# Most of the products with w1 and w3 of four feed-forwards as 2x2 blocks in seven products instead of eight

## The chip, the cores and the metric

One core of one Trainium2 chip runs one decoding step of a four-layer network in float32. The metric is the device time of one execution in microseconds; the median of the runs counts.

## The reference, cut to what matters

Each layer adds a token mixer and then a SwiGLU feed-forward to x. 512 prompt tokens and 8 x 4 sample tokens share the weights, which gives 544 columns. The mixers (convolution, latent attention, retention, convolution) are not changed. The feed-forward is:

```python
D_MODEL, D_FF, DEPTH, EPS = 1024, 2816, 4, 1e-6

def _rmsnorm(x, g):
    xf = x * lax.rsqrt(jnp.mean(x * x, axis=-1, keepdims=True) + EPS)
    return xf * g

def _swiglu(h, w1, w3, w2):
    return (jax.nn.silu(h @ w1) * (h @ w3)) @ w2

for i in range(DEPTH):
    ...                                            # x += mixer(rmsnorm(x))
    x = x + _swiglu(_rmsnorm(x, norm_ffn[i]), ffn_w1[i], ffn_w3[i], ffn_w2[i])
```

## The kernel before, in words

Activations are feature-major: x is 8 tiles (k = 0..7) of 128 features on the partitions by 544 columns, and a matmul takes half of the columns, 272. A float32 operand is split into a high and a low part (`wsplit`, lines 184 and 185, for weights: a cast on ScalarE, ACT in the rows, and a subtraction on VectorE, DVE in the rows; `split`, lines 191 and 192, for activations). A product is three matmuls: high by high, high by low, low by high. `gemm` (line 204) does this for one tile of 128 output features: 8 tiles of k, three parts, two halves of the columns, so 48 matmuls, into a pair of PSUM banks (`duo`, two of them).

`ffn` (line 428 on) works as follows. `enter` and `prep` (lines 224 and 225) make the split parts of x times the gain, without the division by the root mean square; that factor R needs a sum over all features (line 235) and some steps on ScalarE and VectorE (lines 246 to 250), and is multiplied onto each result (`times`, line 280). So the products may start before R is known. The 22 tiles of D_FF are walked in chunks of 8, 8 and 6. For each pair of tiles, 1 MB of w1 and 1 MB of w3 are loaded (`wload`, line 176, on SP's queue, into two buffers `raw`); for each tile, w1 is split and multiplied, then w3; silu (line 453) and the product of the two (line 456) follow, and the result is split into gh and gl. After a chunk, its part of w2 is multiplied with the chunk's g for all 8 tiles of x and added to x (`add_x`, line 284). In the last chunk of the last layer this is done by halves of the columns, with the final norm behind it (lines 473, 379 to 421).

What sets the order of the work: the code issues instructions into a planner (the Tile framework) that keeps dependencies, gives out buffers of the pools, and puts each engine's instructions into one fixed order when the program is built. Instructions of one engine that are ready in its plan run in the program's order; one whose inputs are late lets later ones pass. On the chip each engine then follows that fixed order. Six buffers `ws` hold three pairs of split weights; four scratch buffers `scr` and 16 buffers `xs` (split x) exist.

Of the kernel before, what the change touches and what calls it, by code (L numbers as in the profile page):

```python
# [70 lines left out]
def constants():  # L71
# [29 lines left out]
    # rows (batch, part, token) of the samples: high and low parts of keys and values, each with each  # L101
# [23 lines left out]
class Later:  # L125
    """a value whose instructions are issued at its first use"""
# [10 lines left out]
class Trunk:  # L137
# [4 lines left out]
    @contextmanager  # L142
    def in_order(self, *engines):
        """keeps what the block issues on these engines in its order"""
        tc, cur = self.tc, self.nc.cur_bb
        n = len(cur.bb.instructions)
        yield
        last = {}
        for i in cur.bb.instructions[n:]:
            if i.engine in engines:  # L150
                if i.engine in last:
                    tc.add_manual_dep(i, last[i.engine].name,
                                      mybir.DependencyInfo(mybir.DependencyClass.NoSync, mybir.DependencyReason.DATA),
                                      reason="order")
                last[i.engine] = i
# [6 lines left out]

    def bank(self, name):
        return self.psb.tile([P, 512], F, tag="b", name=name)

# [29 lines left out]
    def gemm(self, ps, wh, wl, xs, M=P, halves=(0, 1), order=None, then=None, hk=None):  # L195
        """ps[:M, half, :272] = sum_k w_k^T x_k"""
# [9 lines left out]

    def enter(self, gcol, order=range(KD), early=0):
        """hi and lo parts of x * g, and 1 / rms over the features"""
# [9 lines left out]
    def prep(self, xin, gcol, order=None):  # L218
        """hi and lo parts of x * g"""
        nc, out = self.nc, {}  # L220
        for k in order or range(len(xin)):
            hi = self.xsp.tile([P, T], FR, tag="xs", name="xh")
            lo = self.xsp.tile([P, T], FR, tag="xs", name="xl")
            nc.scalar.activation(hi, xin[k], AF.Copy, scale=gcol(k))
            nc.vector.scalar_tensor_tensor(out=lo, in0=xin[k], scalar=gcol(k), in1=hi[:, :].bitcast(F),
# [4 lines left out]
    def colsum(self, src):  # L230
        """sums over the partitions, on all of them, as two banks"""
# [7 lines left out]
    def rsqrt(self, v, y, t=None):  # L239
        """y = v ** -0.5"""  # L240
# [11 lines left out]
    def squares(self, xin, acc, order, first=True):  # L252
        """acc += the squares"""
# [10 lines left out]
    def rstat(self, xin, n, pool=None, tag="R", acc=None):  # L264
        """1 / rms over the features, on all partitions"""
# [24 lines left out]
    def run(self):  # L290
        tc, nc, A = self.tc, self.nc, self.A
        with ExitStack() as es:
# [5 lines left out]
            self.xsp = pool("xs", 16)  # L298
# [3 lines left out]
            self.psb = pool("psb", 4, space=bass.MemoryType.PSUM)  # L302
            self.x = self.cst.tile([P, KD, T], F, name="x")
            self.prologue()
            for l, kind in self.layers:
                if kind == 0:
                    self.conv(l, l // 3)
                elif kind == 1:
                    self.mla(l)
                else:  # L310
                    self.ret(l)
# [53 lines left out]
    def finish(self, ep, m, half):  # L365
        """the last norm and the turn to token-major of the m-th 128 features of a half of the tokens"""
# [42 lines left out]
    def last_norm(self, ep, e, half, tiles, t0, w):  # L409
# [3 lines left out]
        # (all rows of the samples' column are written)  # L413
# [14 lines left out]
    def ffn(self, l, last, order):  # L428
        tc, nc, A = self.tc, self.nc, self.A
# [3 lines left out]
        xs, R = self.enter(lambda k: self.col("norm_ffn", l * KD + k), order, EARLY)  # L433
        with ExitStack() as es:
            gp = es.enter_context(tc.tile_pool(name=f"ffn{l}", bufs=16))
            ep = es.enter_context(tc.tile_pool(name="end", bufs=1)) if last else None
            for f0, nf in ((0, 8), (8, 8), (16, 6)):
                gs = []
                for fp in range(0, nf, 2):
                    c0 = (f0 + fp) * P  # L440
                    r1 = self.wload(w1[:, :, c0:c0 + 256], KD, 256)
                    r3 = self.wload(w3[:, :, c0:c0 + 256], KD, 256)
                    for j in range(2):
                        wh, wl = self.wsplit(r1[:, :, j * P:(j + 1) * P], KD, P)
                        p1 = self.duo("p1")
                        self.gemm(p1, wh, wl, xs, order=order, then=R, hk=int(HK[0]))
                        R()
                        wh, wl = self.wsplit(r3[:, :, j * P:(j + 1) * P], KD, P)
                        p3 = self.duo("p3")
                        self.gemm(p3, wh, wl, xs, order=order)  # L450
                        t1 = self.scr("t1")
                        self.times(t1, p1, R)
                        nc.scalar.activation(t1, t1, AF.Silu)
                        t3 = self.scr("t3")
                        self.times(t3, p3, R)
                        nc.vector.tensor_mul(t3, t3, t1)
                        gs.append(self.split(gp, "g", t3, T))
                cuts = ((0, 256), (256, T)) if last and f0 + nf == FF // P else ((0, T),)
                late = None
                for half, (t0, t1) in enumerate(cuts):  # L460
                    for mp in range(0, KD, 2):
                        r2 = self.wload(w2[:, f0:f0 + nf, mp * P:(mp + 2) * P], nf, 256)
                        for j in range(2):
                            wh, wl = self.wsplit(r2[:, :, j * P:(j + 1) * P], nf, P)
                            if len(cuts) == 1:
                                ps = self.duo("p2")
                                self.gemm(ps, wh, wl, gs)
                                self.add_x(mp + j, ps)
                                continue
# [12 lines left out]
    def conv(self, l, j):  # L482
# [5 lines left out]
        with tc.tile_pool(name=f"cv{j}", bufs=1) as cp:  # L488
            # gated inputs: 30 rows of the past and 512 of the prompt; then 34 rows of each sample
# [11 lines left out]
            def taps_and_past():  # L501
# [7 lines left out]
                # tap 4 i + s of channel 32 g + c at partition 4 c + s  # L509
# [52 lines left out]
            # some channels tap by tap on VectorE  # L562
# [35 lines left out]
            # layer norm over the channels, about the mean of 128 of them  # L598
# [10 lines left out]
            def convolved(m, h):  # L609
                """a half of the tokens of a tile of channels, less K, and its part of the sums"""  # L610
# [32 lines left out]
            cs = [tuple(self.xsp.tile([P, T], FR, tag="xs", name="cs") for _ in range(2)) for _ in range(KD)]  # L643
# [982 lines left out]
```

## Time and profile before

| | us |
|---|---|
| median of 3 runs | 2868.93 |
| the three runs | 2868.93, 2869.55, 2865.14 |
| span of the profiled execution | 2899.4 |
| TensorE busy in it | 2836.5 (98%) |
| VectorE busy | 1563.7 (54%) |
| ScalarE busy | 991.3 (34%) |

The profiled execution is 1.1% longer than the median. Its instructions fill the span from the first to the last; the page shows nothing around it. A row of a view has a start or a mean duration in us or ns; on VectorE and ScalarE the next instruction can start a little before the one ahead of it has ended, so the step from start to start is what a full queue costs.

### The profile page before, as it was taken

To read this page: it belongs to the slowest core of one execution; us is meant where nothing else is said; L and a number is where in the kernel's file an instruction comes from. 1 tells how busy PE (TensorE), PEld (TensorE's weight loads), DVE (VectorE), ACT (ScalarE), POOL (GpSimd) and SP (SyncE) were. 2 spreads that over 40 slices of the span, in tenths; PEclk is the share of its full clock that TensorE was granted. 3 is DMA by queue.
4 is the path that set the end of the run, shared out by engine and by line. 5 is a ranking of instruction groups with operands and counts; after the bars stand their busy time and mean duration, and the time that the engine had idled before them with its cause. 6 is when DMAs were issued, how large, how long until landed. Compare 5 with 4: busy or idle time off the path is not lost.

```text
span 2899.4 us, 52901 instructions
## 1 busy us (share of the span) xinstructions
PE 2836.5 (98%) x23158; PEld 2662.8 (92%) x23158; DVE 1563.7 (54%) x2414; ACT 991.3 (34%) x1489; POOL 130.0 (4%) x217
## 2 busy tenths in 40 slices
PE   8989999999899999999999999999999999999998
PEld 7869999997679999999798897999999987999998
DVE  7875434356665434346656565743434796633335
ACT  4244222234454322224534344522223314422225
POOL 1000000012330000000101000000000000000000
PEclk9999999999999999999999999999999999999999
DMA  5453222233232222222524334322222444332323
GB/s 157 113 129 117 89 87 89 87 102 120 82 107 82 86 89 84 87 84 87 199 86 176 121 139 143 111 88 88 88 88 87 119 125 123 103 103 74 102 73 119
DMA packets 253116, 306.74 MB, mean 106 GB/s; under 512 B 14367, under 2 KB 217452, under 8 KB 252854
## 3 DMA queue, kind: packets, MB, share of 16 engines
q1 hardware_dynamic: 241260, 267.88, 29.8%
q0 software_dynamic: 11328, 33.59, 3.4%
q8 instruction: 182, 2.98, 0.4%
q10 hardware_dynamic: 298, 1.88, 0.2%
q14 instruction: 48, 0.39, 0.0%
HBM read 257.56 MB, written 24.01 MB: 97 GB/s over the span
## 4 chain that ended last, share of the span: by engine, by line
PE 94%; DMA 2%; SPq 1%; DVE 1%; ACT 1%; issue 1%; another core or an unknown queue 0%; ACTq 0%
PE p L204 54%; PE pg L204 7%; PE pqk L204 3%; PE pa L204 3%; PE pwo L204 3%; PE cv L621 2%; PE pw L204 2%; PE po L204 2%; PE pd L204 1%; PE pv L1273 1%; PE pv L1274 1%; PE pv L1275 1%; DMA S<-U 1%; PE ob L1508 1%; SPq L585 1%
## 5 line engine op out<-in xcount | busy, mean ns | idle before, releaser
L184 ACT CAST wh<-raw 128x1024 fp32r<-128x1024 f32 (+2 forms) x434 | 436.0, 1006 | 1458.0 <-PE p L204 1025.7
L204 PE MATMUL p<-xl,wh 128*128 128x272 f32 x2816 | 585.8, 290 | 0.0
L204 PE MATMUL p<-xh,wl 128*128 128x272 f32 x2816 | 583.4, 289 | 0.0
L204 PE MATMUL p<-xh,wh 128*128 128x272 f32 x2816 | 582.9, 289 | 0.0
L185 DVE TENSOR_TENSOR wl<-raw,wh 128x1024 fp32r<-128x1024 f32 (+2 forms) x434 | 506.3, 1168 | 94.5 <-ACT wh L184 71.4
L204 PEld LDWEIGHTS p<-xh,wh 128*128 128x128 f32 x2816 | 442.9, 188 | 0.7 <-DVE t L280 0.3
L204 PEld LDWEIGHTS p<-xh,wl 128*128 128x128 f32 x2816 | 443.5, 188 | 0.0
L204 PEld LDWEIGHTS p<-xl,wh 128*128 128x128 f32 x2816 | 441.4, 189 | 0.0
L280 DVE TENSOR_TENSOR t<-p,R 128x544 f32<-128x544 f32 x176 | 127.6, 725 | 570.8 <-PE p L204 570.7
L204 PE MATMUL p<-gl,wh 128*128 128x272 f32 x1312 | 273.0, 289 | 0.0
L204 PE MATMUL p<-gh,wl 128*128 128x272 f32 x1312 | 271.5, 288 | 0.0
L204 PE MATMUL p<-gh,wh 128*128 128x272 f32 x1312 | 271.4, 288 | 0.0
L284 DVE TENSOR_TENSOR x<-p,x 128x544 f32<-128x544 f32 x88 | 63.8, 725 | 279.6 <-PE p L204 279.6
L204 PEld LDWEIGHTS p<-gh,wh 128*128 128x128 f32 x1312 | 206.2, 188 | 0.0
L204 PEld LDWEIGHTS p<-gh,wl 128*128 128x128 f32 x1312 | 206.1, 188 | 0.0
L204 PEld LDWEIGHTS p<-gl,wh 128*128 128x128 f32 x1312 | 205.7, 189 | 0.0
L621 PE MATMUL cv<-S,W 128*32 128x240 f32 (+1 forms) x1408 | 100.1, 399 | 17.7 <-DMA S<-U 14.0
L204 PE MATMUL pg<-xh,wh 128*128 128x272 f32 x512 | 112.1, 295 | 4.1 <-ACT wh L184 4.1
L571 DVE SCALAR_TENSOR_TENSOR cc<-U,taps,cc 128x512 f32<-128x512 f32 (+1 forms) x180 | 113.3, 663 | 1.0
L204 PE MATMUL pg<-xh,wl 128*128 128x272 f32 x512 | 109.6, 292 | 0.0
L204 PE MATMUL pg<-xl,wh 128*128 128x272 f32 x512 | 108.4, 291 | 0.0
L621 PEld LDWEIGHTS cv<-S,W 128*32 128x32 f32 x1408 | 52.6, 115 | 59.5 <-DMA S<-U 23.6
(519 smaller groups left out, 4475.0 us busy)
## 6 DMA issues: line engine op xcount, KB each, us to landing
raw<-in_ffn_w SPq DMA_DIRECT2D x120, 1024.0 KB
raw<-in_conv_w_pw SPq DMA_DIRECT2D x28, 1024.0 KB
state<-in_state_ret SPq DMA_DIRECT2D x32, 512.0 KB
out_ret_state_sample<-state POOLq DMA_DIRECT2D x32, 512.0 KB
raw<-in_ffn_w SPq DMA_DIRECT2D x20, 768.0 KB
S<-U SPq DMA_DIRECT2D x48, 280.0 KB
raw<-in_ret_w_v SPq DMA_DIRECT2D x8, 1024.0 KB
raw<-in_ret_w_g SPq DMA_DIRECT2D x8, 1024.0 KB
```

What stands on the lines that cost most here:

```text
L184: self.nc.scalar.copy(hv, raw)
L185: self.nc.vector.tensor_sub(lv, raw, hv.bitcast(F))
L204: nc.tensor.matmul(ps[:M, h, :HF], lhsT=w[:, k, :], rhs=x[:, h * HF:(h + 1) * HF], start=(j == 0 and i == 0), stop=(j == n - 1 and i == 2))
L280: self.nc.vector.tensor_mul(self.v2(out), ps[:M, :, :HF], self.v2(R[:M, :]))
L284: self.nc.vector.tensor_add(x, ps[:, :, :HF], x)
L571: nc.vector.scalar_tensor_tensor(out=cc[m][:, a:z], in0=U[:, m, k + a:k + z], scalar=taps[:, m, k:k + 1], in1=cc[m][:, a:z], op0=ALU.mult, ...
L585: nc.sync.dma_start(S[:, g, a0 - c0:], bass.AP(src.tensor, src.offset, [list(src.ap[0]), [1, 4], [1, c1 - a0]]))
L621: nc.tensor.matmul(b[g * 32:(g + 1) * 32, :n], lhsT=W[:, g * 8 + i, :], rhs=S[:, g, 4 * i:4 * i + n], start=(i == 0), stop=(i == 7))
L1273: nc.tensor.matmul(out, lhsT=ah, rhs=bh, start=start, stop=False)
L1274: nc.tensor.matmul(out, lhsT=ah, rhs=bl, start=False, stop=False)
L1275: nc.tensor.matmul(out, lhsT=al, rhs=bh, start=False, stop=stop)
L1508: nc.tensor.matmul(s["ob"][q * 32:(q + 1) * 32, :], lhsT=s["qm"][:, e, q * 2 + r, :], rhs=ts[q // 2][:, q % 2, :], start=(q > 0 and r == 0 ...
```

## The change

The 22 tiles of w1 and w3 are now two tiles the old way (`plain`), then five quads of four tiles. In a quad, 512 output features by 1024 features of x by 544 columns are taken as 2x2 blocks: output halves of 256 features, halves of 512 in k, halves of 272 columns. Seven products of blocks (`product`, 24 matmuls each) replace eight (in effect 192 matmuls become 168 for each weight and quad). This is Winograd's form of Strassen's scheme: the weight blocks enter as themselves and as four sums (S, on VectorE, `whole`), each of the seven is split on its own; the blocks of x enter as themselves and as four differences (`less`), also split each on its own, once for a layer (`prepared`). The products are added up in PSUM where the accumulation allows it; three partial results for each weight are copied out by ScalarE (`kept`) and added on VectorE (`gate`, `value`).

Because sums of blocks are split into parts, R can't wait until after the product: x is multiplied with gain and R beforehand for the quads (`normed`, 16 operations of 272 columns), while `plain` still works as before. A quad's weights come as two loads of 1 MB for each of w1 and w3: the first 512 features of k into `raw`, the others into `raw2`, which has one buffer.

w2 now follows each quad (`down`): chunks of 6, 4, 4, 4, 4 tiles instead of 8, 8, 6. Two tiles of x are split and multiplied together, then added. Split x is kept in 8 pairs of buffers instead of 16 single ones, in all layers, and the PSUM pool of single banks is closed between mixer and feed-forward, where it serves as two pairs. Comments are taken out everywhere; nothing else of the mixers changes.

```diff
+            blocks, full = {}, {}
+            def block(dtype, name):
+                return bp.tile([P, 4, HF], dtype, tag="B", name=name, bufs=15)
+            def normed():
+                for j in range(4):
+                    full["B%d" % j] = block(F, "B")
+                r = R()
+                for k in range(KD):
+                    for h in range(2):
+                        hs = slice(h * HF, (h + 1) * HF)
+                        nc.vector.scalar_tensor_tensor(out=full["B%d" % (k // 4 * 2 + h)][:, k % 4, :], in0=self.x[:, k, hs],
+                                                       scalar=g(k), in1=r[:, hs], op0=ALU.mult, op1=ALU.mult)
+            def less(out, a, b):
+                full[out] = block(F, "T")
+                nc.vector.tensor_sub(full[out], full[a], full[b])
+            def parts(c, of):
+                blocks[c] = block(FR, "Bh"), block(FR, "Bl")
+                h, lo = blocks[c]
+                nc.scalar.copy(h, full[of])
+                nc.vector.tensor_sub(lo, full[of], flat(h))
+            def prepared():
+                normed()
+                parts("1", "B0")
+                less("T1", "B1", "B0")
+                less("T3", "B3", "B1")
+                parts("5", "T1")
+                less("T2", "B3", "T1")
+                less("T4", "B2", "T2")
+                for c, of in zip("63724", ("T2", "B3", "T3", "B2", "T4")):
+                    parts(c, of)
+            def weights(w, f):
+                r1 = self.rawp.tile([P, 2048], F, tag="raw", name="raw").rearrange("p (k c) -> p k c", k=4)
+                nc.sync.dma_start(r1, w[:, 0:4, f * P:f * P + 512])
+                r2 = bp.tile([P, 2048], F, tag="raw2", name="raw2").rearrange("p (k c) -> p k c", k=4)
+                nc.sync.dma_start(r2, w[:, 4:8, f * P:f * P + 512])
+                a11, a21, a12, a22 = r1[:, :, :256], r1[:, :, 256:], r2[:, :, :256], r2[:, :, 256:]
+                ...
+                def whole(op, a, b):
+                    t = self.xsp.tile([P, 1024], F, tag="xs", name="S").rearrange("p (k c) -> p k c", k=4)
+                    op(t, a, b)
+                    return t
+                def split(a):
+                    h, lo = ws("ah"), ws("al")
+                    nc.scalar.copy(h, a)
+                    nc.vector.tensor_sub(lo, a, flat(h))
+                    return h, lo
+                yield split(a11)
+                s1 = whole(nc.vector.tensor_add, a21, a22)
+                yield split(s1)
+                s2 = whole(nc.vector.tensor_sub, s1, a11)
+                yield split(s2)
+                yield split(whole(nc.vector.tensor_sub, a12, s2))
+                yield split(whole(nc.vector.tensor_sub, a11, a21))
+                yield split(a12)
+                yield split(a22)
+            def product(out, c, w, first, final):
+                wh, wl = w
+                bh, bl = blocks[c]
+                for t in range(2):
+                    m = slice(t * P, (t + 1) * P)
+                    for i, (a, b) in enumerate(((wh, bh), (wh, bl), (wl, bh))):
+                        for k in range(4):
+                            nc.tensor.matmul(out[:, t, :HF], lhsT=a[:, k, m], rhs=b[:, k, :],
+                                             start=(first and i == 0 and k == 0), stop=(i == 2 and k == 3),
+                                             skip_group_check=True)
+            def four(w, f, put):
+                ...
+                product(x2, "1", next(ws), True, False)
+                s1 = kept(x2, "u1")
+                x3 = self.pair("x3")
+                product(x3, "5", next(ws), True, False)
+                p5 = kept(x3, "p5")
+                product(x2, "6", next(ws), False, False)
+                u2 = kept(x2, "u2")
+                product(x3, "3", next(ws), False, True)
+                put("12", v(x3), u2)
+                product(x2, "7", next(ws), False, False)
+                put("22", v(x2), p5)
+                x1 = self.pair("x1")
+                product(x1, "2", next(ws), True, True)
+                put("11", v(x1), s1)
+                product(x2, "4", next(ws), False, True)
+                put("21", v(x2), None)
+                ...
+                def gate(which, ps, add):
+                    t = at(hidden[int(which[0]) - 1], which)
+                    if add is not None:
+                        nc.vector.tensor_add(t, ps, add)
+                        ps = t
+                    nc.scalar.activation(t, ps, AF.Silu)
+                def value(which, ps, add):
+                    t = at(hidden[int(which[0]) - 1], which)
+                    gh, gl = (at(x, which) for x in G[int(which[0]) - 1])
+                    if add is not None:
+                        v = self.scr("v").rearrange("p (t n) -> p t n", t=2)
+                        nc.vector.tensor_add(v, ps, add)
+                        ps = v
+                    nc.vector.tensor_mul(t, ps, t)
+                    nc.scalar.copy(gh, t)
+                    nc.vector.tensor_sub(gl, t, flat(gh))
+                four(w1, f, gate)
+                four(w3, f, value)
+            def down(f0, gs):
+                ...
+                        w = [self.wsplit(r2[:, :, j * P:(j + 1) * P], nf, P) for j in range(2)]
+                        if not ends:
+                            ps = [self.duo("p2") for j in range(2)]
+                            if mp == 0:
+                                for h in range(2):
+                                    for j in range(2):
+                                        self.gemm(ps[j], *w[j], gs, halves=(h,))
+                            else:
+                                for j in range(2):
+                                    self.gemm(ps[j], *w[j], gs)
+                            for j in range(2):
+                                self.add_x(mp + j, ps[j])
+                ...
+            plain(0, gs)
+            prepared()
+            f0 = 0
+            for f in range(2, FF // P, 4):
+                quad(f, gs)
+                down(f0, gs)
+                f0, gs = f + 4, []
```

## Rows read from the trace of the kernel before

**Rows 1.** The page: busy time of each engine, its share and instructions.
```profile
PE 2836.5 (98%) x23158; PEld 2662.8 (92%) x23158; DVE 1563.7 (54%) x2414; ACT 991.3 (34%) x1489; POOL 130.0 (4%) x217
```

**Rows 2.** Stretches of the first and last feed-forward: us, busy us (instructions) by engine, granted clock, DMA.
```profile
300.00:450.00 150.00, 150.00 (x1197) 150.00 (x1196) 58.32 (x67) 36.05 (x41) 0.00 (x0) 1.00 0.29 92
...
2550.00:2700.00 150.00, 150.00 (x1197) 150.00 (x1196) 58.93 (x66) 36.65 (x42) 0.00 (x0) 1.00 0.27 85
```

**Rows 3.** VectorE in time: start, duration, line; additions to x after 48 matmuls each.
```profile
346.71 0.72 DVE L284 TENSOR_TENSOR x<-p,x 128x544 f32<-128x544 f32 x1 [2.70 <-PE p L204]
...
352.74 0.72 DVE L284 TENSOR_TENSOR x<-p,x 128x544 f32<-128x544 f32 x1 [3.92 <-PE p L204]
```

**Rows 4.** TensorE in time: single-bank accumulation, three parts in turn.
```profile
229.26 0.29 PE L1273 MATMUL pw2h<-cs,wh 128*128 128x272 f32 x1
229.38 0.29 PE L1274 MATMUL pw2h<-cs,wh 128*128 128x272 f32 x1
229.51 0.29 PE L1275 MATMUL pw2h<-cs,wl 128*128 128x272 f32 x1
```

**Rows 5.** VectorE in time, a full queue: the steps of 544 and of 1024.
```profile
413.84 0.73 DVE L456 TENSOR_TENSOR t<-t,t 128x544 f32<-128x544 f32 x1
414.48 1.22 DVE L185 TENSOR_TENSOR wl<-raw,wh 128x1024 fp32r<-128x1024 f32 x1
415.61 0.72 DVE L192 TENSOR_TENSOR gl<-t,gh 128x544 fp32r<-128x544 f32 x1
```

**Rows 6.** Groups by shape: count, then busy us, mean ns of one, idle before.
```profile
L571 DVE SCALAR_TENSOR_TENSOR cc<-U,taps,cc 128x272 f32<-128x272 f32 x60 | 29.7, 495 | 0.3
L184 ACT CAST wh<-raw 128x1024 fp32r<-128x1024 f32 x373 | 391.1, 1050 | 1356.8 <-PE p L204 960.7 <-PE pg L204 81.7 <-PE pqk L204 64.7
L185 DVE TENSOR_TENSOR wl<-raw,wh 128x512 fp32r<-128x512 f32 x9 | 6.1, 683 | 1.1 <-ACT wh L184 0.7 <-issue 0.4
L191 ACT CAST gh<-t 128x544 fp32r<-128x544 f32 x88 | 57.1, 648 | 73.1 <-DVE t L456 71.4 <-issue 1.7
```

**Rows 7.** VectorE in time at the start of the first feed-forward: R's last step.
```profile
252.66 0.78 DVE L225 SCALAR_TENSOR_TENSOR xl<-x,vec,xh 128x544 fp32r<-128x544 f32 x1
253.36 0.72 DVE L250 SCALAR_TENSOR_TENSOR R<-rsq,R 128x544 f32<-128x544 f32 x1
```

**Rows 8.** The first two tiles' stretch in the four layers, columns as in rows 2.
```profile
242.80:267.70 24.90, 24.90 (x196) 24.57 (x195) 16.43 (x22) 14.98 (x21) 4.50 (x9) 1.00 0.41 130
935.60:960.50 24.90, 24.90 (x196) 24.74 (x195) 14.64 (x19) 11.61 (x14) 0.00 (x0) 1.00 0.28 86
...
2484.30:2509.20 24.90, 24.90 (x196) 24.57 (x194) 16.32 (x22) 14.66 (x20) 4.58 (x9) 1.00 0.40 130
```

**Rows 9.** One of those after R, columns as in rows 2.
```profile
254.00:268.00 14.00, 14.00 (x112) 13.83 (x111) 7.29 (x9) 6.20 (x7) 0.00 (x0) 1.00 0.46 150
```

**Rows 10.** TensorE in time after 4.1 us of idleness.
```profile
23.40 0.82 PE L204 MATMUL pg<-xh,wh 128*128 128x272 f32 x2 [4.11 <-ACT wh L184]
...
27.04 0.41 PE L204 MATMUL pg<-xl,wh 128*128 128x272 f32 x2
```

**Rows 11.** Stretches of latent attention around a lowered clock, columns as in rows 2.
```profile
705.00:709.60 4.60, 4.60 (x36) 3.54 (x35) 2.72 (x6) 1.49 (x4) 0.25 (x1) 1.00 0.17 57
709.60:716.40 6.80, 6.80 (x35) 4.01 (x36) 4.82 (x13) 4.47 (x11) 5.15 (x10) 0.50 0.40 131
```

**Rows 12.** SP's queue: one weight load's issue; then the stretch that holds its bytes.
```profile
319.30 0.37 SPq L176 DMA_DIRECT2D raw<-in_ffn_w  x1
320.00:324.00 4.00, 4.00 (x34) 4.00 (x33) 1.23 (x2) 1.59 (x2) 0.00 (x0) 1.00 0.83 262
```

**Rows 13.** TensorE in time: matmuls of two tiles mixed while x's parts come in.
```profile
249.26 0.54 PE L204 MATMUL p<-xh,wh 128*128 128x272 f32 x3
249.64 0.54 PE L204 MATMUL p<-xl,wh 128*128 128x272 f32 x3
```

**Rows 14.** The end of the program, columns as in rows 2.
```profile
2847.00:2889.00 42.00, 41.72 (x335) 41.09 (x333) 28.80 (x54) 27.31 (x53) 0.00 (x0) 1.00 0.35 120
```

More of the change, by code (lines that the diff above doesn't have):

```diff
@@ L161, in scr, with banks, pair @@
         return self.scrp.tile([P, T], F, tag="scr", name=name)
+    @contextmanager
+    def banks(self, duos=False):
+        with self.tc.tile_pool(name="psb", bufs=2 if duos else 4, space=bass.MemoryType.PSUM) as p:
+            self.psb, self.duos = p, duos
+            yield
     def bank(self, name):
+        if self.duos:
+            return self.pair(name)[:, 0, :]
         return self.psb.tile([P, 512], F, tag="b", name=name)
+    def pair(self, name):
+        return self.psb.tile([P, 2, 512], F, tag="b", name=name)
     def duo(self, name):
@@ L432, in ffn @@
         w2 = A["ffn_w2"][l].rearrange("(k p) c -> p k c", p=P)
-        xs, R = self.enter(lambda k: self.col("norm_ffn", l * KD + k), order, EARLY)
+        g = lambda k: self.col("norm_ffn", l * KD + k)
+        xs, R = self.enter(g, order, EARLY)
         with ExitStack() as es:
[L435 to L458, printed above, removed]
@@ new lines, in quad, with at @@
+            def quad(f, gs, between=None):
+                hidden = [self.xsp.tile([P, 2, T], F, tag="xs", name="hid") for _ in range(2)]
+                G = [pair_of_g() for _ in range(2)]
+                def at(x, which):
+                    return x[:, :, (int(which[1]) - 1) * HF:int(which[1]) * HF]
+                def gate(which, ps, add):
[16 more added lines that the diff above has]
+                four(w3, f, value)
+                for gh, gl in G:
+                    gs.extend((gh[:, j, :], gl[:, j, :]) for j in range(2))
@@ L459, in ffn @@
+            def down(f0, gs):
+                nf = len(gs)
+                ends = last and f0 + nf == FF // P
+                ep = None
+                if ends:
+                    qs.close()
+                    es.enter_context(self.banks())
+                    ep = es.enter_context(tc.tile_pool(name="end", bufs=1))
                 late = None
-                for half, (t0, t1) in enumerate(cuts):
+                for half, (t0, t1) in enumerate(((0, 256), (256, T)) if ends else ((0, T),)):
@@ new lines, in down @@
+                        if not ends:
[4 more added lines that the diff above has]
+                                        self.gemm(ps[j], *w[j], gs, halves=(h,))
+                            else:
+                                for j in range(2):
+                                    self.gemm(ps[j], *w[j], gs)
+                            for j in range(2):
+                                self.add_x(mp + j, ps[j])
+                            continue
@@ L641, in convolved @@
                 nc.vector.tensor_add(S2[:, hs], S2[:, hs], q)
-            cs = [tuple(self.xsp.tile([P, T], FR, tag="xs", name="cs") for _ in range(2)) for _ in range(KD)]
+            cs = [self.xpair("cs") for _ in range(KD)]
             def moments(h):
@@ L1135, in sample_products @@
                 def sample_products():
+                    ts = [t[:96, :512].bitcast(F) for _ in range(2) for t in self.xpair("tm")]
                     for c in range(3):
```

80 lines of the change are left out of this document (57 added, 23 removed).

## The prediction

> **What bounds the kernel now.** I read the page's busy times first [rows 1]: TensorE is busy 98% of the span, VectorE 54%, ScalarE 34%. An average hides stages, so the next view is the stretches inside the feed-forwards [rows 2]: there TensorE is busy all 150 of 150 us, at a granted clock of 1.00, while VectorE works 58 to 59 us and ScalarE 36. Nothing but matmuls sets the pace there, and a matmul taken away is time taken away, as long as VectorE and ScalarE, which the change loads, can follow. The pace: two additions to x that each end 48 matmuls start 6.03 us apart [rows 3], so a matmul of 272 columns costs 125.6 ns.
>
> **What is removed.** For each quad and weight 192 matmuls become 168. With two weights, five quads and four layers, 960 fewer: 960 x 0.1256 = 120.6 us. w2 keeps its count. The new products write twelve matmuls in a row into one bank where the old ones alternated between two; the single-bank accumulation of the convolution's last product runs at the same 0.12 to 0.13 us [rows 4], so I take the same pace.
>
> **VectorE and ScalarE in the quads.** A full VectorE queue steps 0.64 us for 544 columns and 1.13 for 1024 [rows 5]. One weight of a quad has four sums and seven subtractions of 1024 elements, 11 x 1.13 = 12.4 us. w1 adds three additions of 544 (1.9), w3 three additions, four products and four subtractions (7.0). So 14.3 and 19.4 us, beside 168 x 0.1256 = 21.1 us of TensorE each. `down` with four tiles: eight subtractions (0.68 [rows 6]) and eight additions to x (0.72 [rows 3]), 11.2 us beside 24.1. ScalarE has seven casts at 1.05, three copies and four functions at about 0.65 [rows 6]: 11.9 us beside 21.1. So no engine takes the place of TensorE on the average, but w3's half of a quad leaves VectorE only 1.7 us of slack. Three pairs of split weights let a split run two products, 6.0 us, ahead; its cast and subtraction need 2.2. That cover is why I cost the sums and splits of a running quad at nothing; if it is gone they cost what the third rival says.
>
> **The start of each feed-forward** is where the cover ends, and here the largest loss lies. The quads need R, and R's last step ends at 254.1 us in the first layer [rows 7]; the two old-style tiles end at 267.7 [rows 8] (the other three layers have the same stretch, 24.9 us). In the 14 us between, VectorE is already busy for 7.3 [rows 9], so 6.7 are free. The new block work: 16 multiplications of 272 columns at 29.7/60 = 0.495 us [rows 6], 7.9 us, and four differences and seven subtractions of 1088 elements, 11 x 1.13 x 1088/1024 = 13.2; in all 21.1 us. Since ready instructions go in program order, all of that stands ahead of the first weight's subtraction (1.2 us). So 21.1 + 1.2 - 6.7 = 15.6 us after the old-style tiles the first product can end; 16 of its 24 matmuls need only the high weight part and take 2.0 us of this, which leaves 13.6. The second product waits for its sum (1.13) and cast (1.05) while 1 us of the first is left: 1.2 more, 14.8. The least that the work allows: until the seventh product VectorE must do 21.1 + 12.4 + 1.9 - 6.7 = 28.7 us where TensorE would need 6 x 3.01 = 18.1, so 10.6 late in any order. The most, if the first product can't run ahead: 17.5. I take 14, nearer to program order, and 4 x 14 = 56 us; 42 to 70 for the range. TensorE stands still and has nothing else to run there.
>
> **After such a stop** TensorE doesn't resume at full pace: after 4.1 us of idleness the 16 matmuls from 23.40 to 27.04 took 3.64 us instead of 2.0 [rows 10], 1.6 lost. In latent attention the granted clock was 0.50, 1.2 of 2.4 GHz, for 6.8 us after a stretch in which TensorE had been busy in the trace at 36 matmuls in 4.6 us, thinner than in the feed-forward [rows 11]; half of that is 3.4 lost. I take 2 for each start, 8 us in all (0 to 14). The Trainium skill, "TensorE: Matmul & The Clock Gate", section "HAM oscillation — how this bites in real kernels", says that gaps in the matmul stream make the chip halve the clock, so that work after each gap starts slow. That speaks against this change, which puts four gaps into a stream that now has none; by it each start would lose the 3.4 us of the lowered stretch, and the sum would be 5.6 us worse.
>
> **Smaller terms.** The second load of a weight, `raw2`, has one buffer: w3's load can be issued only when w1's last split is done, in the fifth of seven products by the count of pairs. A load issued at 319.30 has moved its megabyte by 324 [rows 12], 4.7 us at most, and the first sum on it, cast included, is due about 9 to 10 us after the issue: it fits with some 2 us to spare, less when VectorE is behind. Behind it on SP's queue stands the next quad's load, behind the waiting sum on VectorE the additions that free PSUM. I take 0.4 us in each of the 20 quads, 8 us (0 to 40). `down` begins with the first half of the columns, whose blocks come last: product, cast and subtraction (0.72 + 0.65 + 0.72) behind the last matmul, with 6 ready matmuls (0.75 us) ahead in program order. The other half is ready, and the planner does mix matmuls of two results when one is late: runs of three instead of two in [rows 13]. So zero, and up to 20 x 1.4 = 28 us if it doesn't. At the program's end TensorE is busy 41.7 of 42 us with six tiles [rows 14]; with four, one tile of x for one half takes 1.5 us there and ScalarE needs about 1.4, so 2 us (0 to 4). The mixers' pairs of buffers and the PSUM pool that closes and opens: all old users are done about when the feed-forward starts; zero, at most 1 us for each of eight borders.
>
> **The sum.** 120.6 - 56 - 8 - 8 - 2 = 46.6 us less than the profiled 2899.4, which is its span. Scaled to the median of the runs (2868.93/2899.4): 46 us, so 2823 us.
>
> **Rivals.**
> First, the start is covered as well as the work allows: 42 instead of 56, no loss in the quads, clock or tail. Gain 120.6 - 42 = 78, so 2791 us. For it: ScalarE and TensorE have nothing in the way. Against: it needs weight sums to pass ready block work.
> Second, the quads limp: w3's half comes 2 us late each time because of the one buffer and the 19.4 of 21.1 us on VectorE. 40 instead of 8: gain 15, so 2854 us. For it: the small slack. Against: loads land in under 5 us, and `down` gives VectorE 13 us to recover.
> Third, slower: the plan doesn't run ahead. For five of seven products the chain is sum 1.13, cast 1.05, subtraction 1.13 = 3.3 us and two hand-overs between engines, against 3.0 us of a product. If splits start only one product ahead, each of the 280 products is late by some 0.4 us, 112 us: 2823 + 112 = 2935 us. The point from which it decides is 46/280 = 0.17 us for each product, little. Against it: three pairs, and sums that wait for nothing but a load.
> Fourth, the change doesn't bring the matmuls it says: 6720 matmuls at 10 ns more than before would take back 67 us: about 2890. [Rows 4] speak against it.
>
> **Chances.** Forecast 0.53, first rival 0.20, second 0.16, third 0.09, fourth 0.02. The range 2785 to 2868 takes in the first two rivals and the bounds of the start; it leaves out the third and fourth and the best end. A measurement of this kernel tells 0.2%, about 6 us, from no change. Faster by more than that: the forecast and the first rival, and most of the second, 0.84; within: 0.06, the upper end of the second; slower: 0.10.
>
> **What the profile after would show.** TensorE with 960 fewer matmuls and full stretches inside the later quads; in each layer one idle stretch of 10 to 17 us some 25 us after the feed-forward's start, ended by VectorE (the subtraction of the first weight or of a block), with a lowered clock or slow matmuls behind it; VectorE near 90% in the w3 halves and about 70% over a feed-forward. Idle time at each quad's second product, ended by a DMA or a sum, would be the second rival; idle time at nearly every product, ended by a cast or subtraction, the third. I am wrong if the start's idle stretch is under 8 us, or if later quads lose more than 1 us each.

## The result, and the profile after

The changed kernel takes 2934.29 us (median of 4 runs, 2930.69 to 2938.58) and the kernel before 2869.24 beside it: 1.0231 times as long, interval 1.0217 to 1.0246. It is slower by 65 us, and 111 us above the forecast. The matmuls did go away. Page of the changed kernel, busy time of each engine with its share and instructions, against [rows 1]:

```profile
PE 2766.2 (94%) x22198; PEld 2577.6 (88%) x22198; DVE 1972.5 (67%) x2890; ACT 1216.5 (41%) x1821; POOL 130.2 (4%) x217
```

TensorE has 960 matmuls fewer, as counted, but only 70 us less busy time where 120.6 were due, and its share fell from 98% to 94%. Where that happened is read from the four feed-forwards alone, each from its first matmul to its last. The first of these four stretches of the changed kernel (columns as in [rows 2]: us, busy us and instructions of PE, PEld, DVE, ACT, POOL, then granted clock, DMA share, GB/s), the sum of the four, and then the same sum for the kernel before:

```profile
243.10:661.40 418.30, 385.70 (x2935) 380.77 (x2933) 275.17 (x321) 170.07 (x222) 5.06 (x10) 0.96 0.27 87
...
sum 1672.10, PE 1546.99 PEld 1525.66 DVE 1103.88 ACT 685.05 POOL 10.21; mean PE 386.75 PEld 381.42 DVE 275.97 ACT 171.26 POOL 2.55
```

```profile
sum 1606.50, PE 1606.22 PEld 1604.79 DVE 697.35 ACT 461.37 POOL 10.25; mean PE 401.55 PEld 401.20 DVE 174.34 ACT 115.34 POOL 2.56
```

The stretches grew by 1672.1 - 1606.5 = 65.6 us, which is the whole loss. Their parts: -120.6 for the matmuls; TensorE stands still for 1672.1 - 1547.0 = 125.1 us, before for 0.3; and the matmuls that are left take 1547.0 - (1606.2 - 120.6) = 61.4 us more than their due, at a mean granted clock of 0.95 to 0.96 in the four instead of 1.00. (The profiled execution of before spent 292 us in the latent attention, where a second one spent 266; its longer span was that, and the feed-forwards are alike in both.)

Who ends TensorE's waits, largest first (in total, times, longest):

```profile
PE x L565 <- ACT ah L545: 84.2, 22, 10.3
PE x L565 <- DVE al L546: 26.2, 2, 13.1
...
PE p L216 <- DVE gl L619: 8.7, 34, 0.4
```

These are three places. Two waits of 13.1 (first and last layer) and two of the 22 on `ah`, of 10.3 (the two middle layers), are the starts of the quads; the other 20 waits on `ah` are one in each quad, and the third row is `down`.

**The start of the quads**, first layer: TensorE, then VectorE, then two stretches (start, duration, line, operation, and in brackets the idle time and what ended it):

```profile
270.13 0.77 PE L565 MATMUL x<-Bl,ah 128*128 128x272 f32 x4 [0.34 <-DVE Bl L511]
283.98 1.27 PE L565 MATMUL x<-Bh,al 128*128 128x272 f32 x4 [13.09 <-DVE al L546]
285.06 1.11 PE L565 MATMUL x<-Bh,ah 128*128 128x272 f32 x4
285.96 1.11 PE L565 MATMUL x<-Bl,ah 128*128 128x272 f32 x4
```

```profile
281.51 1.28 DVE L511 TENSOR_TENSOR Bl<-B,Bh 128x1088 fp32r<-128x1088 f32 x1
282.71 1.22 DVE L546 TENSOR_TENSOR al<-raw,ah 128x1024 fp32r<-128x1024 f32 x1
```

```profile
270.90:283.90 13.00, 0.00 (x0) 0.00 (x0) 13.00 (x14) 6.98 (x7) 0.00 (x0) 0.63 0.00 0
283.90:287.90 4.00, 3.92 (x17) 3.92 (x18) 3.97 (x5) 1.33 (x2) 0.00 (x0) 0.50 0.00 0
```

VectorE is busy all 13 us with the blocks of x, and the first weight's subtraction stands behind them, as the prediction had it. The clock falls while TensorE stands and stays at 0.50 (1.2 of 2.4 GHz) for 4 us of work: a group of four starts 0.90 us after the one ahead, 0.226 for a matmul.

**One stop in each quad**, here the second quad of the first layer. VectorE, ScalarE, TensorE and three stretches (the first is that of [rows 2]):

```profile
446.57 1.23 DVE L546 TENSOR_TENSOR al<-S,ah 128x1024 fp32r<-128x1024 f32 x1 [1.53 <-ACT ah L545]
455.01 0.72 DVE L606 TENSOR_TENSOR hid<-x,u 128x544 f32<-128x544 f32 x1 [7.21 <-PE x L565]
455.65 1.21 DVE L540 TENSOR_TENSOR S<-raw 128x1024 f32<-128x1024 f32 x1
```

```profile
455.77 0.66 ACT L608 ACTIVATE hid<-hid 128x544 f32<-128x544 f32 x1 [3.21 <-DVE hid L606]
456.95 1.04 ACT L545 CAST ah<-S 128x1024 fp32r<-128x1024 f32 x1 [0.53 <-DVE S L540]
```

```profile
454.24 0.66 PE L565 MATMUL x<-Bh,al 128*128 128x272 f32 x4
458.05 0.86 PE L565 MATMUL x<-Bh,ah 128*128 128x272 f32 x4 [3.15 <-ACT ah L545]
```

```profile
300.00:450.00 150.00, 145.75 (x1115) 144.48 (x1116) 92.35 (x102) 54.46 (x70) 0.00 (x0) 0.97 0.29 92
...
454.90:458.05 3.15, 0.00 (x1) 0.00 (x1) 1.87 (x3) 1.75 (x3) 0.00 (x0) 1.00 0.01 5
...
458.60:462.00 3.40, 3.40 (x17) 3.40 (x16) 2.93 (x3) 1.29 (x2) 0.00 (x0) 0.50 0.39 133
```

VectorE has nothing to do for 7.21 us. Then, behind the fourth product, comes the first write of `hid` (`put("12")`), and only then the last weight sum, a11 - a21, which needs nothing but weights that have lain there for long. The fifth product waits for that sum and its cast: the step from the last matmul ahead to the first behind, start to start, is 3.43 us in place of 0.13, so 3.3 us are lost (3.65 in two quads of the last layer). The clock is still 1.00 in the stop and 0.50 once the work resumes. All 20 quads have this stop, in w1's half; w3's half has none, and there the same sum runs early. The first row, against the first of [rows 2], has 150 of 150 us busy turned into 145.75 at 0.97.

### The profile page after: what moved, and what is told of

It reads as the page before. It is cut to its first block, busy times and chain, and to the rows that moved or that the text cites. A ratio compares the mean times of both kernels' runs of the same rounds, so it can differ in the third digit from the quotient of the medians.

```text
span 2936.8 us, 52058 instructions
## 1 busy us (share of the span) xinstructions
PE 2766.2 (94%) x22198; PEld 2577.6 (88%) x22198; DVE 1972.5 (67%) x2890; ACT 1216.5 (41%) x1821; POOL 130.2 (4%) x217
## 4 chain that ended last, share of the span: by engine, by line
PE 82%; DVE 10%; ACT 3%; DMA 2%; issue 1%; SPq 1%; ACTq 0%; DVEq 0%
PE x L565 27%; PE p L216 17%; PE pg L216 7%; PE pqk L216 3%; PE pa L216 3%; PE pwo L216 3%; PE pw L216 2%; PE po L216 2%; PE cv L812 1%; DVE gl L619 1%; DMA S<-U 1%; PE pv L1464 1%; PE pv L1465 1%; PE pv L1466 1%; DVE hid L617 1%
## 5 line engine op out<-in xcount | busy, mean ns | idle before, releaser
L196 ACT CAST wh<-raw 128x1024 fp32r<-128x1024 f32 (+3 forms) x338 | 278.1, 826 | 673.4 <-PE p L216 234.1
L565 PE MATMUL x<-Bh,ah 128*128 128x272 f32 x2240 | 398.1, 300 | 84.2 <-ACT ah L545 84.2
L565 PEld LDWEIGHTS x<-Bh,ah 128*128 128x128 f32 x2240 | 336.3, 199 | 89.1 <-ACT ah L545 89.1
L565 PE MATMUL x<-Bh,al 128*128 128x272 f32 x2240 | 386.7, 296 | 26.2 <-DVE al L546 26.2
L565 PE MATMUL x<-Bl,ah 128*128 128x272 f32 x2240 | 386.8, 296 | 0.8 <-DVE Bl L511 0.8
L197 DVE TENSOR_TENSOR wl<-raw,wh 128x1024 fp32r<-128x1024 f32 (+3 forms) x338 | 317.1, 940 | 80.5 <-ACT wh L196 61.2
L565 PEld LDWEIGHTS x<-Bh,al 128*128 128x128 f32 x2240 | 331.0, 197 | 27.1 <-DVE al L546 27.1
L565 PEld LDWEIGHTS x<-Bl,ah 128*128 128x128 f32 x2240 | 330.5, 196 | 1.3 <-DVE Bl L511 1.3
L546 DVE TENSOR_TENSOR al<-S,ah 128x1024 fp32r<-128x1024 f32 x160 | 195.5, 1222 | 83.3 <-ACT ah L545 82.4
L216 PE MATMUL pg<-xs,wh 128*128 128x272 f32 x1024 | 179.1, 293 | 4.9 <-ACT wh L196 4.9
L216 PEld LDWEIGHTS pg<-xs,wh 128*128 128x128 f32 x1024 | 147.7, 190 | 13.1 <-issue 7.3
L546 DVE TENSOR_TENSOR al<-raw,ah 128x1024 fp32r<-128x1024 f32 x120 | 144.5, 1218 | 16.8 <-ACT ah L545 16.4
```

Source lines behind the costliest of these rows:

```text
L196: self.nc.scalar.copy(hv, raw)
L197: self.nc.vector.tensor_sub(lv, raw, hv.bitcast(F))
L216: nc.tensor.matmul(ps[:M, h, :HF], lhsT=w[:, k, :], rhs=x[:, h * HF:(h + 1) * HF], start=(j == 0 and i == 0), stop=(j == n - 1 and i == 2))
L546: nc.vector.tensor_sub(lo, a, flat(h))
L565: nc.tensor.matmul(out[:, t, :HF], lhsT=a[:, k, m], rhs=b[:, k, :], start=(first and i == 0 and k == 0), stop=(i == 2 and k == 3), skip_gr ...
```

## The experiments

The kernel before, once more, for the parts that are not changed:

> The kernel before, for a second trace: its first profiled execution (2899.4 us) is 30 us longer than the median of its runs, with a lowered clock in latent attention. If that is one execution's chance, this span lies near 2868 and latent attention is some 25 us shorter, with the feed-forwards at 399 to 404 us as before; if the profile itself costs it, 2899 again.

It took 2870.17 us. Its four feed-forwards are 399.3, 401.3, 401.3 and 404.4 us long, its mixers as long as those of the changed kernel within 2 us. So the 65 us do lie in the feed-forwards.

**Who holds the sum?** `S` and `hid` come from one pool, `xs`, with one tag and eight buffers. My theory: the planner hands buffers out in the order in which the program first writes them, and since the fourth sum is made only when the fifth product asks for its weights, its first write stands behind that of `hid`. The first run gives `hid` its buffers early, by writing one column of it on GpSimd, and changes nothing else:

```diff
                 hidden = [self.xsp.tile([P, 2, T], F, tag="xs", name="hid") for _ in range(2)]
+                for t in hidden:
+                    nc.gpsimd.memset(t[:, :, 0:1], 0.0)
```

> The two buffers hid of each quad are taken from their pool at the quad's start (one column of each is cleared by GpSimd) instead of by the first addition behind the fourth product; everything else stays. In the changed kernel TensorE stops 3.43 us once in each of the 20 quads, before the fifth product of w1. Theory A, buffers of one pool are handed out in program order, so the sum for the fifth product waited for hid and hid for the fourth product: the 20 stops go, 69 us, and most of the half-clock stretches behind them (about 70 us of half clock, 35 us lost): 2934 - 69 - 35 = 2830, between 2815 and 2850. Rival B, VectorE is too full in the quads (19.4 of 21.1 us): the stops turn up at other products, 2910 to 2934. Rival C, the half clock comes from elsewhere: only the stops go, about 2865.

2832.33 us, 0.987 of before (0.9854 to 0.9887). The same place in VectorE's time (all four sums stand ahead of `hid`), the stretch that answers to the first of [rows 2] with the sum over the feed-forwards, and the page's row of the matmuls that waited for `ah` (last, the idle time before them):

```profile
428.55 1.22 DVE L540 TENSOR_TENSOR S<-raw,S 128x1024 f32<-128x1024 f32 x1
...
431.45 1.22 DVE L540 TENSOR_TENSOR S<-raw 128x1024 f32<-128x1024 f32 x1
...
444.24 0.73 DVE L608 TENSOR_TENSOR hid<-x,u 128x544 f32<-128x544 f32 x1 [1.26 <-PE x L565]
```

```profile
300.00:450.00 150.00, 148.93 (x1182) 147.88 (x1181) 96.06 (x106) 58.16 (x74) 0.41 (x4) 1.00 0.29 96
...
sum 1564.20, PE 1502.76 PEld 1485.66 DVE 1103.16 ACT 683.62 POOL 14.28; mean PE 375.69 PEld 371.42 DVE 275.79 ACT 170.90 POOL 3.57
```

```profile
L565 PE MATMUL x<-Bh,ah 128*128 128x272 f32 x2240 | 374.8, 289 | 20.6 <-ACT ah L545 20.6
```

All 20 stops are gone (the idle time that `ah` ends fell from 84.2 us to 20.6, the starts of the two middle layers), and in the feed-forwards the clock is lowered only at the four starts. Idle time fell by 125.1 - 61.4 = 63.7 us, TensorE's excess by 1547.0 - 1502.8 = 44.2: 5.4 us for each stop of 3.3, because the matmuls behind it ran slow. A shortage of buffers in `xs` is not the cause: here `hid` holds two of the eight for longer, and the stops go. The second run reaches the same end by the other handle, the two sums made ahead of the third split:

```diff
                 s2 = whole(nc.vector.tensor_sub, s1, a11)
+                s4 = whole(nc.vector.tensor_sub, a12, s2)
+                s3 = whole(nc.vector.tensor_sub, a11, a21)
                 yield split(s2)
-                yield split(whole(nc.vector.tensor_sub, a12, s2))
-                yield split(whole(nc.vector.tensor_sub, a11, a21))
+                yield split(s4)
+                yield split(s3)
```

> Nothing is changed in who holds which buffer when, but the third and fourth weight sum of a half are issued before the third product's split, ahead of the first addition that writes hid. Theory A: the same as with hid taken first, within 6 us of it, 2815 to 2850. Rival B, VectorE too full: 2910 to 2934.

2830.45 us, 0.9864 (0.9847 to 0.9881), the same as the first. Two edits that share only the order of first writes to `xs` take the same 102 to 104 us away; that order was the cause.

**What the rest of the change costs.** All 22 tiles the old way, but w2 in the new small chunks:

```diff
-            prepared()
...
-                quad(f, gs)
+                plain(f, gs)
+                plain(f + 2, gs)
```

> All 22 tiles of w1 and w3 the old way, no blocks and no norm beforehand, but with the rest of the change: w2 in chunks of 6, 4, 4, 4, 4 tiles, two tiles of x at a time, pairs of split x, PSUM banks as pairs. TensorE has the 960 matmuls again. Theory A (the loss lies in the quads and the start): 2866 to 2885, the first bound no change, the second 16 stops of 0.76 us at the first product with w2. Rival D, the finer chunks of w2 or the buffers cost much of the loss: 2900 or more.

2888.25 us, 1.006 (1.0043 to 1.0077), above what I expected. The sum over the feed-forwards is

```profile
sum 1623.30, PE 1609.91 PEld 1599.38 DVE 736.82 ACT 471.92 POOL 10.21; mean PE 402.48 PEld 399.85 DVE 184.21 ACT 117.98 POOL 2.55
```

so 16.8 us more than before, 13.1 of it idle time: about 1 us at the beginning of `down`, and the tail, the last layer being 7.5 us longer than the first (411.9 - 404.4) instead of 4.9 (404.3 - 399.4), so 2.6 us. The prediction had put the beginning at zero. In the changed kernel it reads

```profile
417.49 0.39 PE L216 MATMUL p<-gh,wh 128*128 128x272 f32 x1
418.25 0.39 PE L216 MATMUL p<-gl,wh 128*128 128x272 f32 x1 [0.37 <-DVE gl L619]
```

with the halves of the columns in the written order. On top of the second run's edit I put the blocks of x just ahead of the product that needs them (`prepared` keeps only the first block), and in a further run also turned the halves around in `down`:

```diff
             def product(out, c, w, first, final):
+                need(c)                # difference, cast, subtraction of this block
...
-                                for h in range(2):
+                                for h in (1, 0):
```

> On top of the early sums, the difference and the split of each block of x are issued right before the product that needs them, behind that product's weights, instead of all before the first quad. Theory S, the stop of 10.6 to 13.4 us at each feed-forward's start is the order of VectorE's queue (all block work ahead of the first weight): the longest stop falls to about 3 us, the half clock behind it mostly goes, and the time is 4 x (4 to 8) = 15 to 32 us below that of the early sums alone. Rival W, VectorE's total work decides (10.6 us late in any order, by the prediction's sum): TensorE still stands some 9 to 11 us in each start, in several pieces, and the time falls by less than 12 us.

> Early sums and late blocks as before, and at each product with w2 the second half of the columns is multiplied first, since its blocks are finished first. In the run with late blocks TensorE stands 0.76 and 0.46 us (0.97 above the pace) at each of 16 such places. Theory H, the planner keeps the written order of the halves and the stop is the wait for the last block's low part: the stops go, 16 x 1 = 13 to 16 us: about 2802, between 2797 and 2808. Rival, the stop is a wait for a PSUM bank or for w2: the time stays within 4 us of 2817.

The blocks made late: 2816.83 us, 0.9817 (0.9797 to 0.9836). The gain of 13.6 us lies between the two theories: the start was neither a matter of order alone, nor untouched by it. The stop of 13 us broke into pieces:

```profile
278.29 1.27 PE L569 MATMUL x<-Bl,ah 128*128 128x272 f32 x4 [1.75 <-DVE Bl L511]
...
285.89 0.52 PE L569 MATMUL x<-Bh,ah 128*128 128x272 f32 x2 [1.79 <-ACT Bh L510]
...
293.76 0.77 PE L569 MATMUL x<-Bl,ah 128*128 128x272 f32 x4 [1.59 <-DVE Bl L511]
```

With the halves turned as well: 2795.05 us, 0.9744 (0.9731 to 0.9757), 21.8 us less, more than the theory's 13 to 16. The edit bears on 19 of the 20 calls of `down` (the last one of the last layer goes by halves in any case), so 1.1 us each. This version is 2.6% faster than the kernel before. Its feed-forwards:

```profile
sum 1529.70, PE 1497.88 PEld 1485.93 DVE 1101.33 ACT 682.34 POOL 10.25; mean PE 374.47 PEld 371.48 DVE 275.33 ACT 170.58 POOL 2.56
```

76.8 us less than before: -120.6 for the matmuls, 31.5 more idle time, 12.3 of slow matmuls.

**What is left at the start.** In that version VectorE works without a break from 263 to 289 us of the first layer. Three ways to relieve it: two of the subtractions on GpSimd; the seven subtractions left out; each block ahead of its product's weight sums instead of behind them.

```diff
-                nc.vector.tensor_sub(lo, full[of], flat(h))
+                (nc.gpsimd if c in "32" else nc.vector).tensor_sub(lo, full[of], flat(h))
```

> On top of that, two of the seven subtractions for the blocks of x (1088 elements, 1.2 us each on VectorE) run on GpSimd. Theory W, the start is late by VectorE's total work: TensorE's idle time in each start falls by some 2.4 us, and the time by 4 x 2.4 = 8 to 12 us. Rival, order or the cast on ScalarE sets it: within 3 us of the run before it; or slower, if GpSimd takes longer than the block is away (its price isn't on record here).

2796.63 us, 0.9747 (0.9734 to 0.9761): nothing. Here on GpSimd the subtraction took 5.76 us where VectorE takes 1.28 (the eight of this run took 2.65 to 6.82, by a profile that is rough on GpSimd), and the late stop is only ended by another engine:

```profile
283.23 5.76 POOL L511 TENSOR_TENSOR Bl<-B,Bh 128x1088 fp32r<-128x1088 f32 x1 [32.60 <-DVE Bl L511]
```

```profile
289.05 0.77 PE L569 MATMUL x<-Bl,ah 128*128 128x272 f32 x4 [1.24 <-POOL Bl L511]
```

The second way leaves out the low parts of the blocks; `product` multiplies the high part in their place:

```diff
-                blocks[c] = block(FR, "Bh"), block(FR, "Bl")
-                h, lo = blocks[c]
+                h = block(FR, "Bh")
+                blocks[c] = h, h
                 nc.scalar.copy(h, full[of])
-                nc.vector.tensor_sub(lo, full[of], flat(h))
```

> Leaves out the seven subtractions that make the low parts of the blocks of x (the high part is multiplied in their place), 8.4 us of VectorE's work in each start; matmuls, order and the rest stay as with the late half first. Theory W, VectorE's total work makes the start late: the 9.4 to 12.5 us of idle time in each start fall by about 8, and the half clock with them: 4 x (8 to 10) = 30 to 40 us less than the run with the late half first. Rival, the order or ScalarE's casts make it late: less than 12 us.

2783.22 us, 0.9703 (0.9688 to 0.9718): 11.8 us for 34 us of VectorE's work, the rival's size. In its first layer the third and fourth weight sum stand on VectorE ahead of the difference of x blocks whose cast the third product waits for:

```profile
283.82 2.18 PE L568 MATMUL x<-Bh,ah 128*128 128x272 f32 x8 [5.50 <-ACT Bh L510]
```

```profile
279.08 1.22 DVE L540 TENSOR_TENSOR S<-raw 128x1024 f32<-128x1024 f32 x1
...
281.35 1.28 DVE L505 TENSOR_TENSOR T<-B,T 128x1088 f32<-128x1088 f32 x1
```

So the order was tried by itself, together with a way to fill the gap: w2 of the two old-style tiles multiplied ahead of the first quad (in another run). On the chips of these two runs and of the last one the kernel before took 2897 and 2892 us; the ratios count.

```diff
             def product(out, c, w, first, final):
                 need(c)
-                wh, wl = w             # w was next(ws), taken before need(c)
+                wh, wl = next(w)
```

```diff
             prepared()
-            f0 = 0
+            down(0, gs)
+            f0, gs = 2, []
```

> The version with the late half first, and the order of the start turned once more: each product's blocks of x (difference, cast, subtraction) now stand ahead of that product's weight sum and split in program order, not behind them. The amount of VectorE's work is the same. Theory O (what is left of the start is VectorE's order: the third product waits for the cast of a difference that stands behind weight sums): that stop of some 2 us goes from each layer with part of the lowered clock behind it, 8 to 16 us in all, so 2779 to 2787 us. Rival T (VectorE's total work sets it: it works without a break from 263 to 289 us in the first layer): a stop only moves to the products that wait for weights, within 4 us of 2795.

> The version with the late half first, and w2 of the two plain tiles multiplied by itself ahead of the first quad, so that TensorE has 96 matmuls (12 us) while VectorE makes the blocks. Matmuls in all as before; VectorE has eight more additions to x in each layer (5.1 us), which it can spare later. Theory T: the 6.4 to 10.7 us of idleness in each layer and the 6.8 us at half clock are covered for the larger part, 4 x 5 to 4 x 9 us, so 2760 to 2775 us. Rival: the two tiles' results come late themselves (scaling, product, cast and subtraction, some 2.8 us behind the last matmul), and the first quad's loads of w1 stand behind those of w2 in the two buffers, so that the stop moves ahead of the w2 matmuls and the quad starts as late as before: 2790 to 2805 us.

0.9737 (0.972 to 0.9755) and 0.9736 (0.9723 to 0.9749), against 0.9744: the order gains nothing by itself, and neither does the filling (1.2 and 2.9 us in the feed-forwards). Order: the third product now waits for its weight's cast instead of its block's. Filling: the stops moved ahead of w2, whose own inputs are late.

```profile
285.75 1.27 PE L569 MATMUL x<-Bh,ah 128*128 128x272 f32 x4 [1.70 <-ACT ah L546]
```

```profile
273.65 0.36 PE L216 MATMUL p<-gh,wh 128*128 128x272 f32 x1 [1.87 <-DVE t L295]
...
275.00 0.70 PE L216 MATMUL p<-gh,wh 128*128 128x272 f32 x2 [0.73 <-ACT gh L483]
276.49 0.60 PE L216 MATMUL p<-gl,wh 128*128 128x272 f32 x1 [0.79 <-DVE gl L484]
```

Last, the order and the missing subtractions together (the edits are those shown above):

> Both at once: the blocks of x stand ahead of each product's weight sums, and the seven low parts of the blocks aren't made (the high part is used in their place, so the output isn't the reference's). By itself the order changed nothing (0.9737 of before against 0.9744), and the seven subtractions less (8.4 us of VectorE for each layer) gave 12 us (0.9703). Theory T+O (VectorE's amount sets the start, and in the run without the subtractions the order then held back the third product for 4 to 5.5 us): with both, the stop at the third product goes too, another 8 to 20 us, a ratio of 0.963 to 0.9675. Rival (the chain of cast after difference after cast sets the start, whatever stands on VectorE): no more than 4 us beyond the run without the subtractions, 0.969 to 0.972.

0.9682 (0.9665 to 0.9698), between the two expectations. The sums over the feed-forwards, for the order alone, the subtractions left out alone, and both:

```profile
sum 1528.50, PE 1501.29 PEld 1487.27 DVE 1101.18 ACT 681.24 POOL 10.23; mean PE 375.32 PEld 371.82 DVE 275.30 ACT 170.31 POOL 2.56
...
sum 1516.10, PE 1490.85 PEld 1482.63 DVE 1068.77 ACT 682.47 POOL 10.25; mean PE 372.71 PEld 370.66 DVE 267.19 ACT 170.62 POOL 2.56
...
sum 1507.60, PE 1488.73 PEld 1477.87 DVE 1069.16 ACT 682.33 POOL 10.26; mean PE 372.18 PEld 369.47 DVE 267.29 ACT 170.58 POOL 2.56
```

Both together take 8.5 us less than the subtractions left out alone, the lower edge of the theory. In the middle layers the start is then nearly gone (TensorE idle for 3.2 and 1.9 us in their whole feed-forwards). So VectorE's amount of work at the start and its order together hold TensorE back: against the 1529.7 us of the late half first, less work without the order gives 13.6 us, the order without less work 1.2, both 22.1.

## Why the prediction was wrong, by its own steps

- **The matmuls removed** and their pace were right: 960 fewer, and a run without stops goes at the old step. The fourth rival is out.
- **The step that failed is the cover**: "sums and splits of a running quad at nothing", since three pairs let a split run two products ahead. I counted the `ws` buffers and the engines' times, both rightly, and did not ask from which pool the sums themselves come. They share `xs` with `hid`, and one sum of the four waited there for a product. Price: 20 x 5.4 = 108 us of TensorE's time in the feed-forwards, 102 in the measured time. Without it the changed kernel takes 2830 to 2832 us, inside the range and 7 to 9 us above the forecast; that it comes so close is in part luck, since the start and `raw2` were put some 17 us too dear and `down` 22 too cheap.
- **The third rival** gave 2935 and the kernel 2934, but by coincidence: its mechanism is not what happened. It had each of 280 products late by 0.4 us, for a chain of sum, cast and subtraction; here one product in seven of w1's halves is late by 3.3 us, and the chain is fast enough everywhere else. The test that I had set for it, idle time at nearly every product, does not hold; the test "later quads lose more than 1 us each" does.
- **The start** was right in place and mechanism, and nearly in size: steps of 13.4, 10.6, 10.6 and 13.4 us, 47 in all beyond a matmul's step instead of 56, ended by the subtraction in two layers and by a cast in the other two, where the first product had run ahead. That "TensorE stands still and has nothing else to run there" is borne out for the one filling that was tried: w2 of the first tiles is late itself. Two bounds were off. The least, 10.6 us "in any order", is no floor: with late blocks and the halves turned, the feed-forwards of the middle layers have 6.2 and 6.1 us of idle time in all. And the most, 17.5, doesn't come out of the terms beside it (15.6 + 1.2 = 16.8).
- **The clock** at the starts was right: the 16 matmuls from 283.98 took 3.8 us instead of 2.0, and the four starts together lost 7.6 us in their lowered stretches, where 8 were forecast. What was missing is the clock behind the unforeseen stops: 44 of their 108 us by TensorE's busy time, 37 by the steps above 0.1256 us in the lowered stretches alone. The Trainium skill, "TensorE: Matmul & The Clock Gate", section "HAM oscillation — how this bites in real kernels", describes work that starts slow after every gap, each time anew. The trace agrees: 20 stops, and behind each a stretch at 0.50.
- **`raw2`** was put at 8 us and costs none that shows: without the 20 stops no product of w3's half waits. **The second rival** falls with it.
- **`down`** was put at zero, with up to 28 us if the planner does not turn the halves. It does not, and 21.8 us came back when the program did. [Rows 13] showed it mixing two results that were both being fed; that did not carry over to a whole half of the columns that is late by about a microsecond. **The tail**, 2 us, measured 2.6.

With the term for the pool added, the sum is -120.6 + 47 (the starts) + 7 (the clock there, 1.3 to 2.0 us a layer in the first run, from the steps above 0.1256 us in the lowered stretch) + 22 (`down`) + 3 (tail) + 108 = 66 us, against 65.6 in the stretches. A slip in the chances: the third and fourth rival, the slower ones, add up to 0.11, not 0.10.

## What to carry to other kernels

When work is said to run ahead, follow every buffer of its chain and not only the last one: the pool, the tag, how many, and which instruction in program order writes each for the first time; work that is made on demand takes its place in that order late. A cheap probe of such a hold is an early write to the tile that is suspected of standing in front. And price a stop in a dense stream of matmuls above its own length: here 3.3 us of standing still cost 5.4.

## What the runs showed of the hardware

A stop of 3.15 us left the granted clock at 1.00 while it lasted, and then came 3.4 to 6.8 us at 0.50 with TensorE at work, a matmul of 272 columns every 0.226 us instead of 0.1256; behind the stops of 0.4 us in `down` the clock stayed at 1.00 in the first run. A float32 subtraction of 1088 elements took 1.28 us on VectorE and, in the eight cases of one run, 2.65 to 6.82 us on GpSimd.

The latent attention, the same instructions in both kernels, was 266 us long in one profiled run (the late half first) and 294 in another (the blocks ahead of the sums), at a mean granted clock of 0.99 and 0.94:

```profile
624.90:890.90 266.00, 261.61 (x2062) 219.99 (x2060) 177.39 (x383) 135.21 (x300) 74.71 (x95) 0.99 0.37 113
```

```profile
628.60:922.60 294.00, 275.08 (x2062) 230.31 (x2061) 177.74 (x383) 135.72 (x300) 75.11 (x95) 0.94 0.33 103
```

These 28 us are most of the 31 by which the two profiled spans differ. The two ran on different chips, on which the kernel before took 2869 and 2897 us. Why the clock fell there in one and not in the other is open.
